# Head norms broadcast by split float32r products, and the squares of a latent's units added on Pool before one sum over channels

## The chip, the cores and the metric

The kernel runs on one core of a Trainium2 chip. The metric is the device time of one execution in microseconds (us). Engines are named as in the profile: PE is TensorE (PEld its weight loads), DVE VectorE, ACT ScalarE, POOL GpSimd, SP SyncE, which here issues most of the DMAs.

## What is computed

Two transformer-like blocks on one sequence of 1024 tokens with 1024 channels, in float32. The first block is a pooling and state-space mixer with a SwiGLU feed-forward part. The second has a latent attention (MLA) branch and an RWKV-7 branch side by side, gates for both, a feed-forward part and a gated extra input. The change touches two places of the second block. In the reference they are:

```python
h = rmsnorm_2(x, g_mix)
z = h @ w_in
z_mla, z_rwkv, z_gate = jnp.split(z, [MLA_COLS, MLA_COLS + RWKV_COLS], axis=-1)
...
c_q, c_kv, k_pe = jnp.split(z_mla, [384, 640], axis=-1)
q = rmsnorm_2(c_q, g_q_a) @ w_uq
kv = rmsnorm_2(c_kv, g_kv_a) @ w_ukv
...
kk = kk / jnp.maximum(jnp.linalg.norm(kk, axis=-1, keepdims=True), 1e-12)
y = wkv7_scan(r, decay, k, v, -kk, kk * a)
y = (y - mean) * lax.rsqrt(var + GN_EPS)
```

The two latents c_q (384 channels) and c_kv (256 channels) are normalized per token over their channels. In the RWKV branch kk and y are normalized per token over each head's 64 channels; there are 8 heads.

## The kernel before

Channels lie on the 128 partitions and tokens along the free axis. A projection is made in units of 128 output channels: `unit_t` takes a unit's weights (`weights`: a DMA into `wr`, a copy on ACT to `wh`, line 103, and a subtraction on DVE to `wl`, line 104, which split the weights into a high and a low float32r part) and makes 48 matmuls of 128x512 into one two-bank PSUM tile `big`: 8 channel blocks of the normed input `hn`, two halves of the tokens, and three products each (`mm3`, lines 139 to 141). Every matmul of a projection reads `hn`, which sets these matmuls apart in the trace. During the RWKV and attention part PSUM holds two `big`, two `chain` and two `ps` tiles.

`rwkv` first works through the recurrence in four blocks of 256 tokens. For a block i it interleaves three generators: `wkv_prep` (elementwise work on DVE and ACT, then small products that fill the tiles `uv`, `bt`, `at`), `wkv_inverse` (a triangular inverse on DVE in 31 steps, lines 1144 and 1145, between DMA round trips through DRAM: `dg` out and in before it, `dg` and `t11` out and in behind it, lines 1119, 1137, 1147 to 1159) and `wkv_chain` (four links of matmuls, lines 1193 to 1210, each with short copies on ACT and DVE between them and the new state at lines 1212 and 1213). A link reads the state that the link before it left. `wkv_out` normalizes a block's output. Both `wkv_prep` and `wkv_out` call `head_rnorm`, 8 times in all: sums over a head's channels by matmul (line 1011), square root on ACT (1013), maximum and reciprocal on DVE (1014, 1015), and then four float32 matmuls (line 1021) that spread the result, which sits in 2 of 32 rows per channel block, over the 64 channels of each head.

Only behind all four blocks does the program text come to `projections`: 5 units of the two latents, then 16 units of the gates, 21 units or 1008 matmuls on `hn`. For each unit of a latent, ACT copies the PSUM tile out (line 1246, then a DMA to `cl`), squares it (line 1248), and PE sums the squares over the channels by 8 matmuls with a column of ones, token block by token block, into the same PSUM tile (line 1250). DVE copies or adds the 8 columns into `ss` (1253, 1255). After the five units `rsqrt` makes the inverse norms of both latents.

The order of the instructions on each engine is not that of the text. A scheduler of the tile framework moves instructions of each engine ahead where their inputs and buffers are free, and freezes the order when the kernel is built; on the chip each engine works through its list in order. So the projections' matmuls, late in the text, can stand between those of the recurrence. What holds an instruction back is its inputs and its tile's buffer. Buffers are handed out in the order of the text: `slot` takes from one ring of 38 buffers of 1040 columns (tag S), which the recurrence uses throughout; `zo` is a ring of two; `wr`, `wh` and `wl` are rings of two.

```python
def slot(self, name, dt=F32, cols=1024):
    t = self.sp.tile([P, self.SC], dt, tag="S", name=self.nm(name), bufs=self.NS)
...
def zo(self, cols=T):
    return self.wp.tile([P, T + 1], F32, tag="zo", name=self.nm("zo"), bufs=2)[:, 0:cols]
```

Of the kernel before, what the change touches and what calls it, by code (L numbers as in the profile page):

```python
# [9 lines left out]
F32 = mybir.dt.float32  # L10
F32R = mybir.dt.float32r
I32 = mybir.dt.int32
AF = mybir.ActivationFunctionType
ALU = mybir.AluOpType
PSUM = bass.MemoryType.PSUM

P = 128
# [31 lines left out]
class Kernel:  # L49
    def __init__(self, ctx, tc, a):  # L50
        self.tc, self.nc, self.a = tc, tc.nc, a
        nc = self.nc
        self.n = 0
        ent = ctx.enter_context
        self.cp = ent(tc.tile_pool(name="cp", bufs=1))
        self.sp = ent(tc.tile_pool(name="sp", bufs=1))
        self.wp = ent(tc.tile_pool(name="wp", bufs=2))
        self.tp = ent(tc.tile_pool(name="tp", bufs=2))
        self.dp = ent(tc.tile_pool(name="dp", bufs=1, space=bass.MemoryType.DRAM))
        self.NS, self.SC = 38, 1040  # L60
        self.cst = self.cp.tile([P, a["cst"].shape[1]], F32, name="cst")
        self.vec = self.cp.tile([P, NVEC], F32, name="vec")
        self.ident = self.cst[:, 0:128]

# [485 lines left out]
    def block1_mixer(self):  # L550
# [9 lines left out]
        def first_weights():  # L560
            w = [pool_w(0), pool_w(1)]
            for i in range(4, 8):
                (nc.sync, nc.scalar)[i % 2].dma_start(xs[i], a["x"][i * P:(i + 1) * P, :])
            nc.scalar.dma_start(self.cst[:, P:], a["cst"][:, P:])
            return w
        pu = self.norm_units(norm_half, xv, first_weights)
        self.wpl = self.slot("wpl")
# [386 lines left out]
    def rwkv(self, hn):  # L954
        nc, a = self.nc, self.a

        self.dg = self.dp.tile([4, 2, 2, 2, 2, 4, 32, 32], F32, name="dg_wkv")
        self.t11 = self.dp.tile([4, 2, 2, 2, 4, 32, 32], F32, name="t11_wkv")
        self.ybd = self.dp.tile([4, P, T], F32, name="ybd")
        self.oka = self.cp.tile([P, 4], F32, name="oka")  # L960
        nc.vector.tensor_scalar(self.oka, self.vec[:, VOFF["k_a_2"]:VOFF["k_a_2"] + 4], -1.0, 1.0, ALU.mult, ALU.add)
        self.rmask = self.cp.tile([P, 256], F32, name="rmask")
        nc.gpsimd.memset(self.rmask, 1.0)
        nc.gpsimd.memset(self.rmask[:, 0:256:64], 0.0)
        s = self.cp.tile([P, 4, 64], F32, name="wkv_s0")
        nc.gpsimd.memset(s, 0.0)
        self.state = s
        step = lambda g: next(g, None)
        live = [[] for _ in range(4)]
        none = iter(())  # L970
        inv = none
        for i in range(5):
            prep = self.wkv_prep(i, live[i]) if i < 4 else none
            step(prep)
            step(inv)
            chain = self.wkv_chain(live[i - 1]) if i else none
            step(chain)
            step(prep)
            step(chain)
            step(prep)  # L980
            step(inv)
            step(chain)
            step(chain)
            if i < 4:
                inv = self.wkv_inverse(i, live[i])
                step(inv)
            if i:
                self.wkv_out(i - 1, live[i - 1])
        return self.attention(*self.latents(*self.projections(hn)))
# [16 lines left out]
    def head_rnorm(self, x, scale, bias, floor):  # L1006
# [6 lines left out]
        nc.scalar.activation(n, ps[:, 0:256], AF.Sqrt, scale=scale, bias=bias)  # L1013
        nc.vector.tensor_scalar(n, n, floor, None, ALU.max)
        nc.vector.reciprocal(n, n)
        out = []
        for i in range(2):
            ps = self.ps()
            for j in range(2):
                c = 904 + (2 * i + j) * P  # L1020
                nc.tensor.matmul(ps[:, j * 256:j * 256 + 256], lhsT=self.cst[:, c:c + P], rhs=n, start=True, stop=True)  # L1021
            out.append(ps)
        return out

# [211 lines left out]
    def projections(self, hn):  # L1236
# [2 lines left out]
        nc, a = self.nc, self.a  # L1239
        cl = self.dp.tile([5, P, T], F32, name="cl")  # L1240
        ss = self.tiny(16, tag="ss16", bufs=1)
        for j, (o, n, g) in enumerate(self.LATENTS):
            for i in range(n):
                ps = self.unit_t(self.weights(a["w_latent"][o + i]), hn)
                c, sq = self.zo(), self.zo()
                nc.scalar.copy(c, ps)
                nc.sync.dma_start(cl[o + i], c)
                nc.scalar.activation(sq, ps, AF.Square, scale=(n * P) ** -0.5)
                for t in range(8):
                    nc.tensor.matmul(ps[:, t:t + 1], lhsT=sq[:, t * P:(t + 1) * P], rhs=self.cst[:, 260:261], start=True, stop=True)  # L1250
                s = ss[:, 8 * j:8 * j + 8]
                if i == 0:
                    nc.vector.tensor_copy(s, ps[:, 0:8])
                else:
                    nc.vector.tensor_tensor(s, s, ps[:, 0:8], ALU.add)
        rs = self.rsqrt(ss, 16, 1.0, EPS)
        self.gd = self.dp.tile([16, P, T], F32, name="gd")
        for u in range(16):
            ps = self.unit_t(self.weights(a["w_gates"][u]), hn)
            g = self.zo()  # L1260
            nc.scalar.activation(g, ps, AF.Sigmoid)
            nc.sync.dma_start(self.gd[u], g)
            if u == 3:
                ps = self.big()
                nc.tensor.transpose(ps[0:16, 0:P], rs, self.ident)
# [235 lines left out]
```

## Time and profile before

| what | value |
|---|---|
| device time, median of 3 runs | 3022.22 us (3017.02 to 3025.08) |
| the profiled execution, its own time | 3025.18 us |
| its span in the trace | 3023.3 us |
| PE busy | 2899.8 us, 96% |
| DVE, ACT, POOL busy | 1404.1, 825.3, 21.8 us |
| mean granted TensorE clock | 0.978 of full speed |

The span is what the profile's rows cover; the execution's own time is 1.9 us longer. A busy share on PE includes each matmul's pipelined tail, so that a stretch of short matmuls looks fuller than it is. A row of a view of stretches gives the stretch and its length, the busy time (and instructions) of PE, PEld, DVE, ACT and, where all are shown, POOL, then the granted TensorE clock as a share of full speed, the DMA share and GB/s. A row of waits gives the instruction and what released it, the total in us, how often, and the longest. A timeline row gives start, length, engine, instruction and, in brackets, the idle time before it. A group row gives line, engine, operation, tiles as out<-in, shapes and count, then the busy time, the mean duration in ns, and the idle time of the engine just before them with what ended it.

### The profile page before, as it was taken

What the parts mean: (1) busy time and instruction counts of PE and PEld (TensorE: products, weight loads), DVE (VectorE), ACT (ScalarE), POOL (GpSimd) and SP (SyncE); (2) the same over time, 40 slices, a digit from 0 to 9 for tenths busy, and PEclk for the clock granted to TensorE, in tenths of its full rate; (3) what the DMA queues carried; (4) which work ended last, traced back from release to release, by engine and by line L of the source; (5) the groups of instructions that cost most, each with busy time, mean ns of one, the idle gap of its engine ahead of it and who ended that gap; (6) DMA issues with size and microseconds to landing.
All of it is one profiled execution on the core that took longest, in us unless ns stands there. A gap on an engine that the chain in (4) does not pass through costs nothing.

```text
span 3023.3 us, 36716 instructions
## 1 busy us (share of the span) xinstructions
PE 2899.8 (96%) x15289; PEld 2327.6 (77%) x15289; DVE 1404.1 (46%) x2469; ACT 825.3 (27%) x1229; POOL 21.8 (1%) x73
## 2 busy tenths in 40 slices
PE   8989999999999999989788999999999999999998
PEld 6777888888888877867566777777888888888877
DVE  7774422222222462276676436545453333333366
ACT  4242311211121344143342334432131221111142
POOL 0000000000000000000000000000000000000000
PEclk9999999999999998999899999999999999999999
DMA  3344111111111234233232320023211111111122
GB/s 133 105 128 146 35 42 42 63 44 40 42 63 49 73 137 153 105 117 90 69 90 88 98 83 13 29 105 134 75 35 42 42 56 49 56 49 42 42 77 98
DMA packets 126390, 225.37 MB, mean 75 GB/s; under 512 B 52177, under 2 KB 73297, under 8 KB 126225
## 3 DMA queue, kind: packets, MB, share of 16 engines
q1 hardware_dynamic: 117200, 211.00, 21.0%
q10 hardware_dynamic: 9024, 12.04, 1.5%
q8 instruction: 120, 1.97, 0.3%
q14 instruction: 46, 0.37, 0.0%
HBM read 171.48 MB, written 48.23 MB: 73 GB/s over the span
## 4 chain that ended last, share of the span: by engine, by line
PE 87%; DVE 9%; issue 2%; ACT 1%; DMA 1%; ACTq 0%; SPq 0%; DVEq 0%
PE big L139 24%; PE big L140 24%; PE big L141 24%; PE big L822 2%; PE chain L855 2%; DVE tt L1145 2%; DVE wt L1144 2%; PE ps L839 1%; PE ps L1114 1%; PE ps L1021 1%; PE big L192 1%; PE chain L1205 0%; PE chain L139 0%; PE chain L140 0%; PE chain L141 0%
## 5 line engine op out<-in xcount | busy, mean ns | idle before, releaser
L139 PE MATMUL big<-hn,wh 128*128 128x512 f32 x1872 | 745.6, 399 | 8.5 <-DVE zo L914 4.0
L141 PE MATMUL big<-hn,wl 128*128 128x512 f32 x1872 | 742.5, 397 | 5.3 <-DVE wl L104 5.2
L140 PE MATMUL big<-hn,wh 128*128 128x512 f32 x1872 | 744.5, 398 | 1.9 <-DVE hn L197 1.9
L139 PEld LDWEIGHTS big<-hn,wh 128*128 128x128 f32 x1872 | 352.8, 189 | 94.2 <-issue 6.2
L141 PEld LDWEIGHTS big<-hn,wl 128*128 128x128 f32 x1872 | 353.4, 189 | 90.7 <-DVE wl L104 8.4
L140 PEld LDWEIGHTS big<-hn,wh 128*128 128x128 f32 x1872 | 353.0, 189 | 88.0 <-issue 3.2
L103 ACT CAST wh<-wr 128x1024 fp32r<-128x1024 f32 (+1 forms) x142 | 141.9, 1000 | 966.4 <-PE big L140 777.4
L104 DVE TENSOR_TENSOR wl<-wr,wh 128x1024 fp32r<-128x1024 f32 (+1 forms) x142 | 165.0, 1162 | 410.5 <-ACT wh L103 405.7
L140 PE MATMUL big<-wk,a 128*128 128x512 f32 x864 | 338.4, 394 | 0.0
L141 PE MATMUL big<-wk,a 128*128 128x512 f32 x864 | 338.3, 393 | 0.0
L139 PE MATMUL big<-wk,a 128*128 128x512 f32 x864 | 334.9, 396 | 1.8 <-ACT wk L103 1.8
L659 DVE TENSOR_TENSOR r<-big,r 128x1024 f32<-128x1024 f32 x144 | 176.2, 1224 | 318.2 <-PE big L141 318.1
L139 PEld LDWEIGHTS big<-wk,a 128*128 128x128 f32 x864 | 160.9, 188 | 43.8 <-ACT wk L103 7.6
L140 PEld LDWEIGHTS big<-wk,a 128*128 128x128 f32 x864 | 162.2, 188 | 38.8 <-DVE wk L104 0.7
L141 PEld LDWEIGHTS big<-wk,a 128*128 128x128 f32 x864 | 162.2, 188 | 37.6
L674 ACT ACTIVATE zo<-big 128x1024 f32<-128x1024 f32 x32 | 32.8, 1026 | 371.4 <-PE big L141 371.4
L668 DVE TENSOR_TENSOR zo<-zo,big 128x1024 f32<-128x1024 f32 x22 | 26.9, 1221 | 205.2 <-PE big L141 205.2
L104 DVE TENSOR_TENSOR wk<-wr,wk 128x1024 fp32r<-128x1024 f32 (+1 forms) x86 | 100.3, 1171 | 31.1 <-ACT wk L103 31.0
L140 PE MATMUL big<-wk,mx 128*128 128x512 f32 x256 | 102.3, 399 | 1.3 <-DVE wk L104 1.3
L139 PE MATMUL big<-wk,mx 128*128 128x512 f32 x256 | 101.0, 401 | 2.3 <-ACT wk L103 2.3
L141 PE MATMUL big<-wk,mx 128*128 128x512 f32 x256 | 101.6, 397 | 0.0
L675 DVE TENSOR_TENSOR zo<-zo 128x1024 f32<-128x1024 f32 x32 | 39.2, 1225 | 131.7 <-ACT zo L674 131.7
(411 smaller groups left out, 3629.5 us busy)
## 6 DMA issues: line engine op xcount, KB each, us to landing
wr<-in_w_ffn_up_dram SPq DMA_DIRECT2D x32, 512.0 KB, 3.2
wr<-in_w_ffn_down_dram SPq DMA_DIRECT2D x32, 512.0 KB, 3.2
zr<-zo SPq DMA_DIRECT2D x24, 512.0 KB, 3.5
wr<-in_w_gate_dram SPq DMA_DIRECT2D x22, 512.0 KB, 3.3
wr<-in_w_up_dram SPq DMA_DIRECT2D x22, 512.0 KB, 3.2
wr<-in_w_down_dram SPq DMA_DIRECT2D x22, 512.0 KB, 3.2
wr<-in_w_gates_dram SPq DMA_DIRECT2D x16, 512.0 KB, 4.9
gd<-zo SPq DMA_DIRECT2D x16, 512.0 KB, 3.0
```

The costliest lines, as they stand in the source:

```text
L103: nc.scalar.copy(hi, x)
L104: nc.vector.tensor_tensor(lo, x, hi.bitcast(F32), ALU.subtract)
L139: nc.tensor.matmul(ps, lhsT=w[0], rhs=x[0], start=start, stop=False)
L140: nc.tensor.matmul(ps, lhsT=w[0], rhs=x[1], start=False, stop=False)
L141: nc.tensor.matmul(ps, lhsT=w[1], rhs=x[0], start=False, stop=stop)
L659: nc.vector.tensor_tensor(res[t], ps, res[t], ALU.add)
L674: nc.scalar.activation(s, ps, AF.Relu)
L675: nc.vector.tensor_tensor(s, s, s, ALU.mult)
L822: nc.tensor.matmul(sc[:, c:c + m], lhsT=qs[e][:, i * P:(i + 1) * P], rhs=ks[e][:, c:c + m], start=True, stop=True)
L855: nc.tensor.matmul(o, lhsT=pts[t // 4][:, (t % 4) * P:(t % 4 + 1) * P], rhs=vh, start=t == 0, stop=t == i)
L1144: nc.vector.tensor_tensor(t3, d[h, j:j + 1, j + 1:32].to_broadcast([64, n, m]), tt[h, 0:n, j:j + 1].to_broadcast([64, n, m]), ALU.mult)
L1145: nc.vector.tensor_tensor(tt[h, 0:n, j + 1:32], tt[h, 0:n, j + 1:32], t3, ALU.add)
```

## The change

`head_rnorm` splits the reciprocal `n` into a high and a low float32r part (a copy on ACT and a subtraction on DVE, into a tile `rh` of the ring of slots), and spreads both with 8 float32r matmuls in place of 4 float32 ones. The selection matrix moves from the constants into a float32r tile `sel`, loaded through a slot and copied on ACT once. In `projections` each latent gets a slot `sq`. Its first unit's squares go straight into `sq`; those of the others go into a `zo` and are added to `sq` on Pool. Once per latent, behind the next unit's matmuls, 8 matmuls sum `sq` over the channels into a `ps` tile, and DVE copies the 8 columns into `ss`. `rsqrt` comes after the first gate unit.

```diff
--- before.py
+++ after.py
@@ -58,7 +58,8 @@
         self.tp = ent(tc.tile_pool(name="tp", bufs=2))
         self.dp = ent(tc.tile_pool(name="dp", bufs=1, space=bass.MemoryType.DRAM))
         self.NS, self.SC = 38, 1040
-        self.cst = self.cp.tile([P, a["cst"].shape[1]], F32, name="cst")
+        self.cst = self.cp.tile([P, 904], F32, name="cst")
+        self.sel = self.cp.tile([P, 512], F32R, name="sel")
         self.vec = self.cp.tile([P, NVEC], F32, name="vec")
         self.ident = self.cst[:, 0:128]
 
@@ -561,7 +562,7 @@
             w = [pool_w(0), pool_w(1)]
             for i in range(4, 8):
                 (nc.sync, nc.scalar)[i % 2].dma_start(xs[i], a["x"][i * P:(i + 1) * P, :])
-            nc.scalar.dma_start(self.cst[:, P:], a["cst"][:, P:])
+            nc.scalar.dma_start(self.cst[:, P:], a["cst"][:, P:904])
             return w
         pu = self.norm_units(norm_half, xv, first_weights)
         self.wpl = self.slot("wpl")
@@ -957,6 +958,9 @@
         self.dg = self.dp.tile([4, 2, 2, 2, 2, 4, 32, 32], F32, name="dg_wkv")
         self.t11 = self.dp.tile([4, 2, 2, 2, 4, 32, 32], F32, name="t11_wkv")
         self.ybd = self.dp.tile([4, P, T], F32, name="ybd")
+        raw = self.slot("sel", cols=512)
+        nc.sync.dma_start(raw, a["cst"][:, 904:1416])
+        nc.scalar.copy(self.sel, raw)
         self.oka = self.cp.tile([P, 4], F32, name="oka")
         nc.vector.tensor_scalar(self.oka, self.vec[:, VOFF["k_a_2"]:VOFF["k_a_2"] + 4], -1.0, 1.0, ALU.mult, ALU.add)
         self.rmask = self.cp.tile([P, 256], F32, name="rmask")
@@ -1013,12 +1017,17 @@
         nc.scalar.activation(n, ps[:, 0:256], AF.Sqrt, scale=scale, bias=bias)
         nc.vector.tensor_scalar(n, n, floor, None, ALU.max)
         nc.vector.reciprocal(n, n)
+        h = self.slot("rh", F32R)
+        hi, lo = h[:, 0:256], h[:, 256:512]
+        self.split(n, hi, lo)
         out = []
         for i in range(2):
             ps = self.ps()
             for j in range(2):
-                c = 904 + (2 * i + j) * P
-                nc.tensor.matmul(ps[:, j * 256:j * 256 + 256], lhsT=self.cst[:, c:c + P], rhs=n, start=True, stop=True)
+                c = (2 * i + j) * P
+                o = ps[:, j * 256:j * 256 + 256]
+                nc.tensor.matmul(o, lhsT=self.sel[:, c:c + P], rhs=hi, start=True, stop=False)
+                nc.tensor.matmul(o, lhsT=self.sel[:, c:c + P], rhs=lo, start=False, stop=True)
             out.append(ps)
         return out
 
@@ -1239,27 +1248,35 @@
         nc, a = self.nc, self.a
         cl = self.dp.tile([5, P, T], F32, name="cl")
         ss = self.tiny(16, tag="ss16", bufs=1)
+        def total(j, sq):
+            ps = self.ps()
+            for t in range(8):
+                nc.tensor.matmul(ps[:, t:t + 1], lhsT=sq[:, t * P:(t + 1) * P], rhs=self.cst[:, 260:261], start=True, stop=True)
+            nc.vector.tensor_copy(ss[:, 8 * j:8 * j + 8], ps[:, 0:8])
+        later = []
         for j, (o, n, g) in enumerate(self.LATENTS):
+            sq = self.slot("sq")
             for i in range(n):
                 ps = self.unit_t(self.weights(a["w_latent"][o + i]), hn)
-                c, sq = self.zo(), self.zo()
+                while later:
+                    total(*later.pop())
+                c = self.zo()
                 nc.scalar.copy(c, ps)
                 nc.sync.dma_start(cl[o + i], c)
-                nc.scalar.activation(sq, ps, AF.Square, scale=(n * P) ** -0.5)
-                for t in range(8):
-                    nc.tensor.matmul(ps[:, t:t + 1], lhsT=sq[:, t * P:(t + 1) * P], rhs=self.cst[:, 260:261], start=True, stop=True)
-                s = ss[:, 8 * j:8 * j + 8]
-                if i == 0:
-                    nc.vector.tensor_copy(s, ps[:, 0:8])
-                else:
-                    nc.vector.tensor_tensor(s, s, ps[:, 0:8], ALU.add)
-        rs = self.rsqrt(ss, 16, 1.0, EPS)
+                s = self.zo() if i else sq
+                nc.scalar.activation(s, ps, AF.Square, scale=(n * P) ** -0.5)
+                if i:
+                    nc.gpsimd.tensor_tensor(sq, sq, s, ALU.add)
+            later.append((j, sq))
         self.gd = self.dp.tile([16, P, T], F32, name="gd")
         for u in range(16):
             ps = self.unit_t(self.weights(a["w_gates"][u]), hn)
             g = self.zo()
             nc.scalar.activation(g, ps, AF.Sigmoid)
             nc.sync.dma_start(self.gd[u], g)
+            if u == 0:
+                total(*later.pop())
+                rs = self.rsqrt(ss, 16, 1.0, EPS)
             if u == 3:
                 ps = self.big()
                 nc.tensor.transpose(ps[0:16, 0:P], rs, self.ident)
```

Lines of the changed file from `wkv_prep` to `wkv_out` are 9 higher than before: 1148 becomes 1157, 1176 becomes 1185, 1201 becomes 1210, 1205 to 1210 become 1214 to 1219, 1212 and 1213 become 1221 and 1222. The lines of the split (103, 104) and of `mm3` (139 to 141) become 104, 105 and 140 to 142.

**On ACT, the squares of the latents.** Before, the second unit of the first latent: its copy and its square follow the cast of its weights (an `L1246`, an `L1248`), and the next unit's cast comes next.

```order
L103 CAST wh_11216<-wr_11214 128x1024
L1246 COPY zo_11131<-big_11082 128x1024
L1248 ACTIVATE zo_11132<-big_11082 128x1024
L103 CAST wh_11285<-wr_11283 128x1024
L1246 COPY zo_11200<-big_11151 128x1024
```

Now the square of the first unit of the first latent, tile `sq_11136` out of the PSUM tile `big_11143`, stands here, behind the last link of the fourth block and the last head norm:

```order
L1211 COPY uv_10359<-chain_11059 64x4x64
L1223 COPY tt_10586<-chain_11070 128x4x64
L1234 ACTIVATE ysq_11101<-tt_10586 128x1024
L1017 ACTIVATE rn_11108<-ps_11103,cst 128x256
L104 CAST rh_11112<-rn_11108 128x256
L1267 ACTIVATE sq_11136<-big_11143 128x1024
```

The square has moved behind the whole recurrence. The copy of that same PSUM tile, `zo_11192<-big_11143`, still stands 134 rows further ahead. The squares of the second and third unit stand ahead too, in the two `zo` buffers.

**On PE, the last link of the fourth block.** Before, matmuls of a gate unit on `hn` stand between the matmuls of the link:

```order
L1199 MATMUL chain_11006<-xs_11004,at_10365 64x64 x8
L140 MATMUL big_12091<-hn_7101,wh_12087 128x512
L141 MATMUL big_12091<-hn_7101,wl_12088 128x512
L139 MATMUL big_12149<-hn_6980,wh_12145 128x512
L1205 MATMUL chain_11017<-uv_10313,bt_10335 64x64
L140 MATMUL big_12149<-hn_6980,wh_12145 128x512
L141 MATMUL big_12149<-hn_6980,wl_12146 128x512
L139 MATMUL big_12149<-hn_6981,wh_12145 128x512
L140 MATMUL big_12149<-hn_6981,wh_12145 128x512
L1205 MATMUL chain_11017<-uv_10313,bt_10335 64x64 x7
L1208 MATMUL chain_11017<-at_10365,uv_10313 64x64 x8
L1210 MATMUL chain_11017<-ar_10056,wst_10983 64x64 x8
```

Now the link's matmuls follow one another and the head norm:

```order
L1208 MATMUL chain_11059<-xs_11057,at_10411 64x64 x8
L1214 MATMUL chain_11070<-uv_10359,bt_10381 64x64 x8
L1217 MATMUL chain_11070<-at_10411,uv_10359 64x64 x8
L1219 MATMUL chain_11070<-ar_10102,wst_11036 64x64 x8
L1015 MATMUL ps_11103<-ysq_11101,cst 32x256 x4
L1029 MATMUL ps_11115<-rh_11112,sel 128x256
```

Seven more rows of lines 1029 and 1030 follow, and only then the next matmuls on `hn`:

```order
L1030 MATMUL ps_11120<-rh_11112,sel 128x256
L140 MATMUL big_11394<-hn_6981,wh_11390 128x512
L141 MATMUL big_11394<-hn_6981,wh_11390 128x512
L142 MATMUL big_11394<-hn_6981,wl_11391 128x512
L140 MATMUL big_11394<-hn_6982,wh_11390 128x512
L141 MATMUL big_11394<-hn_6982,wh_11390 128x512
```

Counted over the lists, of the 1008 matmuls of the 21 units before, 194 stand ahead of the second block's line 1002 (behind that block's head norm), 654 between there and the last matmul of line 1021, and 160 behind it. Now 192 (four units) stand ahead of that line, none between there and the last matmul of line 1030, and 816 (17 units) behind it. The latents' sums over channels (now line 1254) stand among these: 8 behind the first 8 matmuls on `hn`, 8 behind 88 more.

**On DVE, behind the inverse of the second block** (`tt` is its result, its column copy the last work of the inverse). Before, elementwise work for the third block follows (lines 1066, 1069, 1081), with small steps of `rsqrt`; one weight split comes next and then the copies of line 1176 and 1201 that belong to the second block's chain:

```order
L1148 COPY tt_9094<-tt_9094 128x512
L1066 TENSOR_TENSOR ar_9332<-kk_9298,P_9292 128x4x2x64
L1066 TENSOR_TENSOR ar_9333<-kk_9298,P_9292 128x4x2x64
L1069 TENSOR_TENSOR ar_9333<-r_9330,P_9292 128x4x2x64
L160 SCALAR_TENSOR_TENSOR t_11430<-t_11427,t_11423 128x16
L157 TENSOR_TENSOR t_11432<-t_11430,t_11425 128x16
L158 TENSOR_TENSOR t_11432<-t_11432,t_11430 128x16
L160 SCALAR_TENSOR_TENSOR t_11435<-t_11432,t_11430 128x16
L157 TENSOR_TENSOR t_11437<-t_11435,t_11425 128x16
L158 TENSOR_TENSOR t_11437<-t_11437,t_11435 128x16
L160 SCALAR_TENSOR_TENSOR t_11440<-t_11437,t_11435 128x16
L1081 TENSOR_TENSOR r_9330<-r_9330,km_9299 128x1024
```

Now the head norm of the third block comes there, then at once the copies and the new state of the chain's first link (lines 1185, 1210, 1221, 1222). The elementwise work stands behind them, and so do lines 1065 and 1066 of the change (1056 and 1057 before):

```order
L1157 COPY tt_9112<-tt_9112 128x512
L1080 COPY dP_9370<-P_9317 128x16
L1018 TENSOR_SCALAR rn_9335<-rn_9335 128x256
L1019 RECIPROCAL rn_9335<-rn_9335 128x256
L105 TENSOR_TENSOR rh_9339<-rn_9335,rh_9339 128x256
L1062 TENSOR_TENSOR kk_9323<-kk_9323,ps_9342 128x512
L1062 TENSOR_TENSOR kk_9323<-kk_9323,ps_9347 128x512
L1185 COPY at_8792<-chain_9396 32x4x32 x2
L1210 COPY uv_8757<-chain_9454 64x4x64
L1185 COPY at_8809<-chain_9396 32x4x32 x2
L1221 TENSOR_TENSOR wst_9490<-chain_9465,wst_9107 128x256
L1222 TENSOR_TENSOR wst_9490<-wst_9490,dP_8633 128x256
```

## Rows read from the trace of the kernel before

**Rows 1.** Page, part 1.

```profile
PE 2899.8 (96%) x15289; PEld 2327.6 (77%) x15289; DVE 1404.1 (46%) x2469; ACT 825.3 (27%) x1229; POOL 21.8 (1%) x73
```

**Rows 2.** Three stretches, matmuls on hn alone.

```profile
1220.00:1260.00 40.00, 40.00 (x175) 32.45 (x174) 0.00 (x0) 0.00 (x0) 1.00 0.32 118
1380.00:1732.00 352.00, 176.90 (x657) 120.74 (x658) 0.00 (x0) 0.00 (x0) 0.93 0.30 88
1732.00:1770.00 38.00, 36.58 (x159) 29.36 (x157) 0.00 (x0) 0.00 (x0) 1.00 0.30 106
```

**Rows 3.** Seven stretches of the recurrence, all instructions.

```profile
1380.00:1425.00 45.00, 44.93 (x712) 35.24 (x713) 21.28 (x57) 12.53 (x31) 1.14 (x6) 0.96 0.33 93
1425.00:1480.00 55.00, 38.41 (x157) 27.68 (x155) 48.68 (x139) 22.63 (x31) 0.00 (x0) 0.81 0.29 81
1480.00:1524.00 44.00, 43.74 (x633) 34.62 (x633) 20.69 (x40) 14.68 (x30) 1.01 (x5) 1.00 0.30 84
1524.00:1580.00 56.00, 41.33 (x255) 31.30 (x252) 48.77 (x145) 23.61 (x32) 0.13 (x1) 0.91 0.25 68
1580.00:1634.00 54.00, 53.96 (x749) 42.08 (x748) 28.52 (x61) 17.31 (x37) 1.01 (x5) 1.00 0.39 125
1634.00:1682.00 48.00, 35.78 (x151) 27.81 (x150) 37.54 (x119) 11.42 (x14) 0.00 (x0) 0.86 0.24 66
1682.00:1732.00 50.00, 50.00 (x639) 37.41 (x638) 14.36 (x28) 14.41 (x26) 0.00 (x0) 1.00 0.31 101
```

**Rows 4.** The stretches of the chains among these, matmuls on hn alone.

```profile
1380.00:1425.00 45.00, 12.54 (x36) 6.47 (x37) 0.00 (x0) 0.00 (x0) 0.96 0.33 93
...
1480.00:1524.00 44.00, 17.36 (x61) 10.77 (x61) 0.00 (x0) 0.00 (x0) 1.00 0.30 84
...
1580.00:1634.00 54.00, 24.13 (x89) 15.44 (x88) 0.00 (x0) 0.00 (x0) 1.00 0.39 125
...
1682.00:1732.00 50.00, 31.05 (x111) 19.26 (x110) 0.00 (x0) 0.00 (x0) 1.00 0.31 101
```

**Rows 5.** What DVE waited for from 1380 to 1732 us: total us, times, longest.

```profile
DVE wst L1212 <- PE chain L1210: 24.7, 13, 3.0
...
DVE uv L1201 <- PE chain L1199: 17.6, 9, 3.1
```

**Rows 6.** Groups from 1280 to 1735 us: the links' short steps.

```profile
L1201 DVE COPY uv<-chain 64x256 f32<-64x256 f32 x16 | 6.8, 428 | 17.8 <-PE chain L1199 17.6
...
L1213 DVE TENSOR_TENSOR wst<-wst,dP 128x256 f32<-128x256 f32 x16 | 6.8, 423 | 0.5
...
L1196 ACT COPY xs<-chain 128x256 f32<-128x256 f32 x16 | 6.0, 373 | 20.3 <-PE chain L1194 20.3
L1202 ACT COPY uv<-chain 64x256 f32<-64x256 f32 x16 | 5.8, 365 | 29.4 <-DVE uv L1201 29.4
```

**Rows 7.** Group of the weights' subtraction on DVE from 1380 to 1732 us.

```profile
L104 DVE TENSOR_TENSOR wl<-wr,wh 128x1024 fp32r<-128x1024 f32 x15 | 18.3, 1221 | 25.7 <-ACT wh L103 21.7 <-DMA t_wkv<-tt 4.0
```

**Rows 8.** Timeline of DVE behind the third block's inverse: start, us, instruction, idle before.

```profile
1569.92 0.64 DVE L1148 COPY tt<-tt 128x512 f32<-128x512 f32 x1
...
1586.67 0.60 DVE L1176 COPY at<-chain 32x128 f32<-32x128 f32 x2 [2.95 <-PE chain L1174]
```

**Rows 9.** Stretches of 3 us around a head norm in the second inverse.

```profile
1443.00:1446.00 3.00, 0.00 (x0) 0.00 (x0) 2.66 (x12) 1.33 (x2) 0.00 (x0) 0.89 0.00 0
...
1452.00:1455.00 3.00, 3.00 (x14) 1.56 (x13) 2.53 (x6) 1.32 (x3) 0.00 (x0) 0.50 0.51 149
1455.00:1458.00 3.00, 1.69 (x10) 0.58 (x3) 2.78 (x8) 2.97 (x4) 0.00 (x0) 0.90 0.17 70
```

**Rows 10.** Groups from 1280 to 1735 us: the two places that the change rewrites.

```profile
L1021 PE MATMUL ps<-rn,cst 128*128 128x256 f32 x64 | 24.5, 549 | 43.0 <-DVE rn L1015 43.0
...
L1250 PE MATMUL big<-cst,zo 128*128 128x1 f32 x80 | 10.1, 256 | 2.7 <-ACT zo L1248 2.7
```

**Rows 11.** Group of the whole span: Pool's copies.

```profile
L784 POOL COPY kh<-kpe 64x512 f32<-64x512 f32 x16 | 10.5, 665 | 287.1 <-DMA kpe<-rope 162.2 <-PE ps L839 74.0 <-PE chain L855 50.2
```

## The prediction

> **What bounds the kernel now.** I read part 1 of the page first [rows 1]: PE is busy for 96% of the span, so whatever takes work off PE or leaves PE empty is what counts. Then the order of the instructions, since the change is small in the text and large there. Then the stretches where the order differs, 1380 to 1732 us, once for all instructions and once for the matmuls on `hn` alone, and last DVE's waits, the groups and the clock in them.
>
> In a stretch with nothing but projection work PE takes 40 us for 175 matmuls on `hn`, 0.2286 us each at a granted clock of 1.00 [rows 2]. From 1380 to 1732 us it also makes 657 of them, as fillers between the recurrence's own work [rows 2]. That stretch alternates [rows 3]: in 1425 to 1480, 1524 to 1580 and 1634 to 1682 the inverse keeps DVE busy for 48.7 of 55, 48.8 of 56 and 37.5 of 48 us, and PE has little else than fillers. In the four others the chains run and DVE is at most half busy. There 36, 61, 89 and 111 fillers stand [rows 4], 297 in all, so about 360 lie in the inverses. The recurrence is thus bound by DVE in one half and by the links of the chain, back and forth between PE, ACT and DVE, in the other. The fillers ride along.
>
> **The change, part by part.** *The fillers leave.* The first square of the first latent now writes into a slot of the ring that the recurrence uses, and in the order of ACT it stands behind the last head norm. Until then its PSUM tile and both `zo` buffers stay taken, so no further unit can be made. On PE 816 matmuls on `hn` stand behind the recurrence where 160 stood: 656 x 0.2286 = **+150.0 us**, all of it exposed, as the 160 before ran at 38 us with PE full [rows 2].
>
> *What the recurrence gets back.* Bounds: nothing, or everything that the fillers could cost it, 297 x 0.2286 = 68 us in the chains and the fillers' 15 weight splits on DVE, 18.3 us [rows 7]. Between links PE would wait anyway: a link passes an ACT copy of 0.373, a DVE copy of 0.428, an ACT copy of 0.365 and two DVE steps of 0.42 us, 2.0 us in which its own matmuls can't go on [rows 6]. By the order of the last links some 12 fillers, 2.7 us, stand in each link. The surplus of 0.7 us over 16 links is -11 us. That DVE waits 24.7 us in 13 waits and 17.6 us in 9, 1.9 us each, for these matmuls [rows 5] fits relays and not queues of fillers. Of the 15 splits about five fall into idle time, as the 25.7 us in front of this group say [rows 7]; ten are on DVE's way, 10 x 1.22 = -12 us. Behind an inverse, 16 us pass from line 1148 to the first copy of line 1176 [rows 8]; they are DMAs out and in, and fillers stand on PE in front of the chain's first matmul. I take 2 us off for each of three blocks, -6 us (bounds 0 and -12).
>
> *DVE's order.* Behind an inverse DVE did elementwise work for the next block while the DMAs ran. Now it does a head norm there and then waits at the copies of the chain, and lines 1056 and 1057 come between the first two links: two instructions of 128x1024, 1.22 us each by the nearest row [rows 7], in two blocks, +5 us. The lower bound is 0 (the wait of 16 us is not full either way), the upper one +16, if all elementwise work of two blocks is pushed behind the first link.
>
> *The clock.* Without fillers PE stands still for most of each inverse. In 1443 to 1446 us PE did nothing and the granted clock was 0.89 on its way down; in 1452 to 1455 it was full of work at 0.50, the lower level of 1.2 GHz, and it was back at 0.90 only in the next 3 us [rows 9]. So a restart costs some 3 us of work done in 6. I count six restarts: four chains, and two more where DVE's elementwise work stops PE behind a first link: **+18 us**. The bounds: 0, as fillers ran at the lower level before too (0.81 to 0.91 in the inverses [rows 3]); and +108 us, if the chains' own PE time, (44.9 - 12.5) + (43.7 - 17.4) + (54.0 - 24.1) + (50.0 - 31.1) = 107.6 us [rows 3, 4], all ran at half speed.
>
> The Trainium skill speaks against the change here: TensorE: Matmul & The Clock Gate, HAM oscillation, says that an engine that waits between short runs of matmuls falls back to the lower clock each time, again and again. By that the chains would run slow throughout, the +108 us in place of +18; it is a rival below. The trace agrees on the fall behind an idle stretch [rows 9], while the clock is 0.96 to 1.00 over the chains as they are, with fillers in them [rows 3].
>
> *The head norms.* The 64 passes of line 1021 took 549 ns each [rows 10], 8 passes for a norm. Now there are 8 float32r passes of the same 256 columns; the nearest rows are the 0.2286 us of a float32r matmul of 512 columns [rows 2] and the 549 ns as they are, so a norm saves 0 to 3 us of PE. It pays a copy on ACT (0.373 us, same size [rows 6]) and a subtraction on DVE (0.423 us, the two-input step of that size [rows 6]), with their hand-overs some 1 us. PE waits 43.0 us for the reciprocal in all [rows 10] because DVE takes it up late within the inverse, and that doesn't change. In the four places where DVE waits for the products, -1 and +1 cancel: 0 us (bounds -12 and +8).
>
> *The sums.* Before, 80 passes took 10.1 us and PE waited 2.7 us for squares [rows 10], mostly inside inverses and so free. Now 32 passes, 4 us by the same 256 ns with pipelining unchanged, stand in the exposed end; against those that were on the way before, +2 us. The first sum waits for the square (some 1 us) and two adds on Pool. Pool's only copies of float32 take 0.665 us for 64x512 [rows 11], so 1.33 us for 1024 columns with one input; two inputs cost between that and the double of it. I take 2 us: 1 + 2 x 2 us against eight matmuls of 0.23 and the norm's own products, +2 us (bounds 0 and +6). If this cover were gone, it would still be under 6 us.
>
> The Trainium skill, GPSIMD Engine Reference, section Elementwise, puts a two-input float32 add at about twice VectorE's time; with the 1.22 us above that would be an estimated 2.4 us for an add, and the sum would be 1 us more. No row here shows such an add.
>
> The sum goes from the profiled execution's 3025.2 us, 3.0 above the median of 3022.2: 3025.2 + 150.0 - 11 - 12 - 6 + 5 + 18 + 0 + 2 + 2 = **3173 us**. A measurement of this kernel can tell 0.3%, 9 us, from no change.
>
> **The rivals.** *The recurrence was held up by its fillers.* Then all 68 and 18 us and the 12 us behind the inverses come back and the clock costs little: 3025 + 150 - 98 + 10 = 3087 us. For it: PE reads as full in the chains [rows 3]. Against it: a busy share there contains pipelined tails, and the relays of 2 us a link remain.
>
> *The clock stays low in the chains* (the rule above). +108 in place of +18: 3263 us. For it: rows 9. Against it: in the chains PE's own short matmuls fill 107.6 of 193 us now, and a larger part once the fillers are out.
>
> *The recurrence falls to DVE's own time* (the other side: not slower). DVE is the engine with most work of its own there: 219.8 us, the sum of DVE in rows 3, less 18.3 for the splits and plus some 5, 206 us. If every wait went with the fillers, the stretch would shrink from 352 to 206 us and give back 146 us: 3025 + 150 - 146 + 4 = 3033 us, at the edge of no change. It decides once the stretch is under some 210 us. Against it: relays and DMA round trips, 16 us behind each inverse, are untouched by fillers.
>
> *The fillers stay, as the text alone suggests.* Then only the sums' 10 + 3 us and half of line 1021's 24.5 us could go: 3025 - 25 = 3000 us. It asks for a free slot at the first square. The order on ACT and PE speaks against it, and an engine's list is fixed.
>
> **How the numbers follow.** The forecast, which takes in about 40 us to either side: 0.72. Fillers on the way (3060 to 3125): 0.12. Clock low (3225 to 3290): 0.11. DVE's own time: 0.03, of which 0.02 within 0.3% and 0.01 above. Fillers stay: 0.02, faster. The range of 8 in 10 leaves out the ends of both outer rivals: 3110 to 3240 us. Faster 0.02, the same 0.02, slower 0.96.
>
> **What would show it.** In the profile after: a stretch of some 350 us from the second block's line 1002 with no matmul on `hn`, PE well under half busy in the inverses and the clock at the lower level there; a run of about 187 us behind it, PE full at 1.00, against 38 before; DVE's time between inverses as before; the wait for the first sum of a few us. The forecast is wrong if matmuls on `hn` appear between the chains' links, if the stretch without them is under 300 us, or if the chains show the lower clock throughout.

## The result and the profile after

The changed kernel takes 3186.3 us (median of 4 runs, 3183.6 to 3187.6) against 3023.7 us before: ratio 1.054 (95% interval 1.052 to 1.056). That is inside the range of 3110 to 3240 and 13 us above the forecast. The profiled execution took 3187.3 us, its span is 3185.5 us.

Part 1 of the page after, in answer to [rows 1]:

```profile
PE 2924.7 (92%) x15241; PEld 2362.3 (74%) x15241; DVE 1407.5 (44%) x2474; ACT 816.1 (26%) x1228; POOL 29.3 (1%) x76
```

The matmuls on `hn` alone in stretches of the kernel after, in answer to [rows 2]:

```profile
1220.00:1260.00 40.00, 40.00 (x175) 32.47 (x174) 0.00 (x0) 0.00 (x0) 1.00 0.28 105
1380.00:1732.00 352.00, 1.06 (x5) 0.74 (x4) 0.00 (x0) 0.00 (x0) 0.62 0.18 47
1732.00:1960.00 228.00, 192.05 (x816) 154.47 (x814) 0.00 (x0) 0.00 (x0) 0.97 0.28 95
```

The recurrence has lost its fillers (5 matmuls where 657 were), and 816 stand behind it. The seven stretches of the kernel after with all instructions, in answer to [rows 3]:

```profile
1380.00:1425.00 45.00, 36.11 (x542) 29.31 (x541) 19.16 (x35) 11.72 (x29) 1.01 (x5) 0.76 0.22 57
1425.00:1480.00 55.00, 11.27 (x151) 8.36 (x149) 44.47 (x145) 14.90 (x23) 0.13 (x1) 0.56 0.17 43
1480.00:1524.00 44.00, 34.80 (x489) 28.38 (x490) 22.02 (x39) 12.49 (x31) 1.01 (x5) 0.63 0.22 59
1524.00:1580.00 56.00, 12.18 (x198) 9.70 (x196) 45.24 (x147) 11.76 (x20) 0.13 (x1) 0.64 0.17 45
1580.00:1634.00 54.00, 40.71 (x560) 32.84 (x562) 27.11 (x45) 15.08 (x36) 1.01 (x5) 0.65 0.22 54
1634.00:1682.00 48.00, 9.29 (x140) 7.33 (x134) 39.15 (x137) 5.49 (x11) 0.00 (x0) 0.59 0.15 40
1682.00:1732.00 50.00, 34.80 (x530) 30.02 (x531) 10.96 (x26) 8.96 (x21) 1.43 (x1) 0.50 0.14 33
```

PE is nearly empty in the inverses, and the granted clock is 0.50 to 0.76 throughout. DVE's waits in the same 352 us, in answer to [rows 5], did not shrink with the fillers:

```profile
DVE wst L1221 <- PE chain L1219: 31.2, 11, 3.5
DVE at L1185 <- PE chain L1183: 29.0, 10, 7.8
DVE uv L1210 <- PE chain L1208: 25.9, 13, 3.7
```

So the stretch kept its length. The starts of DVE's 16 state steps (line 1212 before, 1221 after) mark the links. The table is worked out from them: the three steps between the four of a block make a block's links, the three gaps from a block to the next hold the inverses, and the last column runs from the last state step to the first matmul of line 756 (757 after), where attention begins.

| kernel, us | links of blocks 1 to 4 | their sum | gaps | first to last | last to attention |
|---|---|---|---|---|---|
| before | 24.3, 33.6, 40.2, 23.9 | 122.0 | 202.1 | 324.1 | 45.8 |
| after | 35.6, 43.6, 45.5, 27.3 | 152.0 | 172.8 | 324.8 | 206.4 |
| e1, norms alone | 39.4, 43.4, 43.4, 23.1 | 149.3 | 199.8 | 349.1 | 14.6 |
| e2, sums alone | 25.8, 30.7, 46.3, 20.3 | 123.1 | 173.8 | 296.9 | 201.4 |
| e3, own buffer | 36.5, 41.6, 41.5, 21.5 | 141.1 | 192.8 | 333.9 | 158.8 |
| x1, after, early | 21.4, 30.1, 29.2, 26.0 | 106.7 | 184.3 | 291.0 | 205.9 |
| x2, norms, early | 26.4, 30.3, 30.3, 23.8 | 110.8 | 208.8 | 319.6 | 33.5 |
| x3, both, early, 37 slots | 28.5, 31.6, 29.5, 23.4 | 113.0 | 218.8 | 331.8 | 36.3 |
| y1, both, early, 38 slots | 23.7, 30.6, 30.3, 23.9 | 108.5 | 213.3 | 321.8 | 33.5 |
| y3, before, early | 24.5, 29.4, 29.0, 23.0 | 105.9 | 201.5 | 307.4 | 58.5 |
| z1, before, 37 slots | 27.7, 43.5, 44.1, 23.3 | 138.6 | 201.4 | 340.0 | 26.7 |

From before to after the gaps fell by 29.3 us, the links grew by 30.0, and the way to attention grew by 160.6. The first state step stayed at 1398.6 us, and behind the start of attention the spans differ by 0.9 us. The table leaves out the time up to the first state step, which comes 8 to 17 us later than before in e1, x2, x3, y1, y3 and z1. Each row is one profiled execution: those of e2 and e3 are 6 us below their medians, those of y1 and z1 6 and 7 us above, so a difference of a few us between rows is not a reading. Of the two parts, the gain in the gaps came with the sums (e2) and the longer links with the norms (e1).

### The profile page after: what moved, and what is told of

Its sections match the earlier page's. It is cut to its first block, busy times and chain, and to the rows that moved or that the text cites. A ratio compares the mean times of both kernels' runs of the same rounds, so it can differ in the third digit from the quotient of the medians.

```text
span 3185.5 us, 36658 instructions
## 1 busy us (share of the span) xinstructions
PE 2924.7 (92%) x15241; PEld 2362.3 (74%) x15241; DVE 1407.5 (44%) x2474; ACT 816.1 (26%) x1228; POOL 29.3 (1%) x76
## 4 chain that ended last, share of the span: by engine, by line
PE 84%; DVE 10%; ACT 3%; issue 2%; DMA 1%; ACTq 0%; POOL 0%; DVEq 0%; SPq 0%; POOLq 0%
PE big L140 24%; PE big L141 23%; PE big L142 23%; PE big L823 2%; DVE tt L1154 2%; DVE wt L1153 2%; PE chain L856 2%; PE ps L840 1%; PE ps L1123 1%; PE big L193 1%; PE chain L1214 0%; PE chain L1208 0%; PE chain L1203 0%; PE ps L1006 0%; PE chain L1202 0%
## 5 line engine op out<-in xcount | busy, mean ns | idle before, releaser
L669 DVE TENSOR_TENSOR zo<-zo,big 128x1024 f32<-128x1024 f32 x22 | 26.9, 1221 | 205.3 <-PE big L142 205.3
L105 DVE TENSOR_TENSOR wk<-wr,wk 128x1024 fp32r<-128x1024 f32 (+1 forms) x86 | 100.3, 1172 | 33.7 <-ACT wk L104 33.6
L1029 PE MATMUL ps<-rh,sel 128*128 128x256 f32 x32 | 12.2, 430 | 105.6 <-ACT rh L104 105.6
```

Of the source, the lines that this page charges most:

```text
L105: nc.vector.tensor_tensor(lo, x, hi.bitcast(F32), ALU.subtract)
```

## The experiments

**The two parts apart.** e1 is the change without its new `projections`; e2 is the new `projections` in the kernel before.

> The head norms' part of the change alone; the latents' squares go to zo and are summed in the unit's own big, as before. In its order 686 matmuls on hn stand between the first and the last link and 55 behind (before: 623 and 187; after: 0 and 816). Theory (the place of the 656 matmuls is what costs): 132 fewer matmuls behind the recurrence are -30 us, 69 more in front of the first link cost 0 to +16 us, so 2995 to 3015 us and no slowdown at all. Rival (the split norms themselves lengthen the recurrence, by a copy, a subtraction and a hand-over in each of four norms): over 3040 us.

Measured 3036.9 us, ratio 1.0046 (1.0031 to 1.0061): slower by 14 us, though 132 fewer matmuls stand behind. Neither number was met. The recurrence is 25 us longer, all of it in the links, as the rival had it; whether by the norms' own work, which was the rival's reason, or by the order is asked by x1 and x2.

> The sums' part of the change alone, head norms as before. In its order 42 matmuls on hn stand between the first and the last link and 816 behind. Theory: this part alone holds back the fillers, so the time is that of the changed kernel, 3186 us, within 15. Rival (the norms cost or save something of their own): under 3160 or over 3210 us.

Measured 3158.5 us, ratio 1.0446 (1.0430 to 1.0462): the rival's side, by 1.5 us. The sums make 136 us of the 163, and the norms some 28 on top. Without fillers the gaps are 28 us shorter, the links not at all.

What the norms did is in DVE's timeline of block 2, from its first state step to the second. First the kernel after:

```profile
1492.27 0.42 DVE L1221 TENSOR_TENSOR wst<-chain,wst 128x256 f32<-128x256 f32 x1 [2.81 <-PE chain L1219]
...
1493.07 1.28 DVE L1075 TENSOR_TENSOR ar<-kk,P 128x512 f32<-128x512 f32 x2
...
1499.65 1.23 DVE L1065 TENSOR_TENSOR km<-km,k 128x1024 f32<-128x1024 f32 x1 [1.09 <-ACT km L999]
...
1501.93 0.68 DVE L1087 TENSOR_TENSOR bk<-km,sg 64x512 f32<-64x512 f32 x1
...
1507.15 1.23 DVE L1090 TENSOR_TENSOR r<-r,km 128x1024 f32<-128x1024 f32 x1
1508.41 0.42 DVE L1221 TENSOR_TENSOR wst<-chain,wst 128x256 f32<-128x256 f32 x1
```

Then e2, with the head norms as before:

```profile
1473.01 1.23 DVE L1081 TENSOR_TENSOR r<-r,km 128x1024 f32<-128x1024 f32 x1 [1.77 <-ACT r L995]
...
1482.12 0.68 DVE L1077 TENSOR_TENSOR bk<-a,sg 64x512 f32<-64x512 f32 x1
...
1487.35 1.29 DVE L1084 TENSOR_TENSOR bv<-ps,v 128x512 f32<-128x512 f32 x2
1488.55 0.41 DVE L1212 TENSOR_TENSOR wst<-chain,wst 128x256 f32<-128x256 f32 x1
...
1501.25 0.42 DVE L1212 TENSOR_TENSOR wst<-chain,wst 128x256 f32<-128x256 f32 x1 [2.87 <-PE chain L1210]
```

In e2 the elementwise steps of the next block are done before the first state step, many while the DMAs behind the inverse run. In the kernel after all of them, `ar` to `r`, stand between the first and the second state step, which are 16.1 us apart. In the order of PE all 32 masked products that need them (line 1123) follow between the second and the third state step, 21.5 us apart; in e2 16 stand there and 16 in the interval before, 10.9 and 12.7 us.

**What holds the fillers.** e3 gives the sum of squares a buffer of its own; the ring pays for it with one slot. e4 also puts the totals into `big` (the last two lines).

```diff
-        self.NS, self.SC = 38, 1040
+        self.NS, self.SC = 37, 1040
-            sq = self.slot("sq")
+            sq = self.tp.tile([P, T], F32, tag="sqo", name=self.nm("sq"), bufs=1)
...
-            ps = self.ps()
+            ps = self.big()
```

> The changed kernel with the sum of squares in a buffer of its own (the ring has 37 slots instead of 38 to make room). In its order 192 matmuls on hn come back between the links and 576 stand behind, since the tile ps of the first total is still handed out behind the recurrence. Theory (two gates stand one behind the other, and the number of matmuls behind sets the time): 240 x 0.2286 = 55 us less than the changed kernel, 3131 us, within 15. Rival (the slot sq is the only thing that bars the fillers): 3000 to 3025 us.

Measured 3150.7 us, ratio 1.0422 (1.0406 to 1.0439). Two gates it is, and the last column fell by 48 us; but the recurrence became 9 us longer with the fillers back in it and one slot fewer, so the time lies 4.7 us above the range.

> The kernel of the run before with the totals in big as well, so that no tile of the latents comes from a ring of the recurrence. In its order 686 matmuls on hn stand between the links and 55 behind, as in the run with the norms alone. Theory: the whole slowdown goes, 2995 to 3015 us. Rival (Pool's adds, the later totals or the norms cost something on the way): over 3040 us.

Measured 3036.3 us, ratio 1.0048 (1.0031 to 1.0065), as e1. Of the 816 matmuls 55 are left behind the recurrence, and 150 us are back. What remains is what e1 has too.

**The order of DVE's steps.** The first step of each block's preparation is put ahead of all other work when the order is made. x1 does this to the changed kernel, x2 to e1, x3 to e4, y3 to the kernel before.

```diff
-            step(prep)
+            with self.tc.high_priority():
+                step(prep)
```

> The changed kernel, its 816 matmuls on hn behind the recurrence as they are, but the first stage of each block's preparation (loads, head norm, the elementwise steps to bv) is put ahead of all other work where the order of the engines is made. In its order the steps ar, km, al, bk, r and bv stand on DVE in front of the chain's first link again, and the second link has 16 of the masked products instead of 32. Theory (the split norms cost 28 us because they push DVE's elementwise steps and PE's masked products in between the links, not by their own work): links and time fall back to those of the sums alone, 3150 to 3165 us, with the sum of the links near 125 us instead of 152. Rival (the split's own copy, subtraction and products cost it, or the clock does): 3175 us or more, links over 140 us.

Measured 3150.5 us, ratio 1.0424 (1.0410 to 1.0437): at the lower end of what the theory had, with 816 matmuls behind as in the kernel after. The links went further down than the 125 us expected, to 106.7, since the third block, which is long in e2 and before too, became short as well; the gaps grew by 11.5 us. The split norms are in x1 as they are in the kernel after, so the longer links of blocks 1 to 3 come with the order and not with the norms' own work. DVE's timeline of block 2 in x1 has `r` and `bv` ahead of the first state step again, and the next state step 10.7 us later:

```profile
1477.01 1.22 DVE L1091 TENSOR_TENSOR r<-r,km 128x1024 f32<-128x1024 f32 x1
...
1482.06 0.69 DVE L1094 TENSOR_TENSOR bv<-ps,v 128x512 f32<-128x512 f32 x1 [0.95 <-PE ps L1007]
...
1486.30 0.42 DVE L1222 TENSOR_TENSOR wst<-chain,wst 128x256 f32<-128x256 f32 x1 [2.50 <-PE chain L1220]
...
1496.96 0.42 DVE L1222 TENSOR_TENSOR wst<-chain,wst 128x256 f32<-128x256 f32 x1 [2.87 <-PE chain L1220]
```

> The head norms alone (the run with +14 us), with the preparation's first stage put ahead as in the run before. 137 matmuls on hn stand behind the recurrence (before: 187), 31 more ahead of the first link. Theory: first to last link falls from 349 to some 320 us and the time to 3000 to 3020 us, no slower than the kernel before. Rival (the split norms cost by themselves): 3030 us or more.

Measured 3017.8 us, ratio 0.9982 (0.9973 to 0.9991), 5 us under the kernel before and the only run whose interval lies below 1. The norms' cost is gone, though the first state step comes 11 us later than before.

> Both parts of the change, with sq in a buffer of its own, the totals in big, and the preparation's first stage put ahead. 149 matmuls on hn behind the recurrence. Theory: neither of the two costs is left, 3000 to 3020 us; against the run with the norms alone the sums save up to 48 passes, at most 6 us. Rival (Pool's adds and late totals cost on the way): 3030 us or more.

Measured 3035.7 us, ratio 1.0041 (1.0029 to 1.0053): a miss. Two runs ask whether the sums or the missing slot did it. y1 is x3 with 38 slots: the sum stays in the first unit's `zo`. y2 is the sums alone in that form.

```diff
-            sq = self.slot("sq")
+            sq = None
-                s = self.zo() if i else sq
+                s = self.zo()
+                sq = sq if i else s
```

> Both parts of the change with the preparation's first stage put ahead, as in the run x3, but the sum of squares stays in the zo buffer of the latent's first unit, so the ring keeps its 38 slots; totals in big. 137 matmuls on hn behind the recurrence, as in x2. Theory (x3 missed by 15 to 35 us because of its 37 slots, with which loads and preparation start later, not because of the sums): 3010 to 3025 us, within 6 us of x2. Rival (Pool's adds and the late totals cost on the way): 3030 us or more.

Measured 3020.7 us, ratio 0.9996 (0.9987 to 1.0005): no different from the kernel before, within 3 us of x2, as the theory had it.

> The sums' part alone in that form: head norms as before, sum of squares kept in zo, totals in big, 38 slots. 187 matmuls on hn behind the recurrence, just as before. Theory (the sums cost 136 us only by the two rings that they take from): 3010 to 3027 us, no difference from the kernel before or a few us less. Rival: 3035 us or more.

Measured 3028.3 us, ratio 1.0017 (1.0008 to 1.0026), 1.3 us over the range and 6 us above the kernel before. 130 of the 136 us are gone; the deferred sums bring nothing.

> The kernel before with a ring of 37 slots instead of 38 and nothing else, so neither split norms nor Pool sums. In its order DVE's steps ar, km, al, bk and r of the last two prepared blocks stand behind the chain's first link and all 32 masked products in the second link, as they do in the changed kernel; 104 matmuls on hn stand behind the recurrence (before: 187). Theory (one slot fewer gives the same long links as the split norms did, which is the cost that x3 had left): the second and third prepared block's two long links take 35 to 38 us each instead of 24.5 and 32.9, the time is 3025 to 3040 us although 83 matmuls, 19 us, fewer stand behind. Rival (the order on DVE and PE in the links does not matter, only the matmuls behind): 3000 to 3010 us.

Measured 3022.6 us, ratio 0.9996 (0.9986 to 1.0006). The links are as expected (36.3 and 36.9 us in blocks 2 and 3), with no split norm in the kernel. The time is 2.4 us under the theory's range and far from the rival's: 16 us of longer links eat most of the 19 us that fewer matmuls behind were worth, and the first state step comes 8 us later. So one slot fewer is enough for long links. Whether the split norms lengthen them because `rh` takes a slot, too, was not tried. The cost that x3 had left is not this one: x3's links are short, 113.0 us against 110.8 in x2, and its gaps are 10 us longer. That the missing slot made x3's 15 us is argued from y1 alone, which also puts the sum elsewhere; the cause stays open.

> The kernel before with the preparation's first stage put ahead and nothing else. 242 matmuls on hn behind the recurrence, 55 more than before. It tells whether the 5 us that x2 is below the kernel before are the norms' or the order's. Theory (the order's): links 12 us shorter, 55 x 0.2286 = 13 us more behind, so 3015 to 3030 us, and x2 is then the split norms' by at most some 10 us. Rival (the split norms are worth nothing once the order is right): within 3 us of x2's 3018.

Measured 3030.7 us, ratio 1.0026 (1.0015 to 1.0036). Links shorter by 16 us, way to attention longer by 12.7, and the first state step 11 us later: 0.7 us above the range. x2 is 13 us lower, but it also has 105 matmuls fewer behind; what the split norms save by their own work was not separated.

**The clock.** The last block's links hold no other block's preparation, and the same instructions ran in them at both clock levels. The second and third of them, all instructions, before (with 12 and 15 fillers):

```profile
1706.00:1714.80 8.80, 8.80 (x174) 6.68 (x174) 2.45 (x8) 1.87 (x5) 0.00 (x0) 1.00 0.01 4
1714.80:1722.70 7.90, 7.90 (x110) 5.79 (x111) 2.48 (x5) 2.98 (x5) 0.00 (x0) 1.00 0.07 28
```

After, no fillers:

```profile
1704.60:1714.80 10.20, 8.78 (x162) 7.65 (x160) 2.39 (x7) 1.87 (x5) 0.00 (x0) 0.50 0.01 2
1714.80:1723.40 8.60, 6.51 (x94) 5.72 (x94) 1.31 (x4) 1.11 (x3) 0.00 (x0) 0.50 0.01 2
```

e2, no fillers either, with its first link ahead:

```profile
1671.90:1679.00 7.10, 5.16 (x98) 4.60 (x100) 1.28 (x3) 1.11 (x3) 0.00 (x0) 0.76 0.35 116
1679.00:1686.20 7.20, 5.49 (x162) 4.58 (x162) 2.46 (x8) 1.87 (x5) 0.00 (x0) 1.00 0.01 2
1686.20:1692.20 6.00, 3.91 (x94) 3.30 (x94) 1.26 (x4) 1.11 (x3) 0.00 (x0) 1.00 0.01 3
```

Without fillers a link takes 6.0 to 7.2 us at the upper level and 8.6 to 10.2 at the lower: 2.6 and 3.0 us for the clock. The fillers cost 1.6 and 1.9 us a link. x4 adds work in the gaps of these links to the changed kernel; nothing uses its products.

```diff
+            warm = lambda x: [nc.tensor.matmul(wp[:, 0:256], lhsT=self.ident, rhs=x, start=True, stop=True) for wp in ([self.ps()] if nwarm else []) for _ in range(nwarm)]
...
+            warm(xs)
```

> The changed kernel with three float32 products of 128x256 added behind each of the three steps of each link of the last block's chain; they read what the step has just made, nothing uses them, and the order of everything else stays. They make PE work in the gaps of the links. Theory (the last block's links take 8.5, 10.2 and 8.6 us and not 7.1, 7.2 and 6.0 as in the run with the sums alone because the clock was at its lower level in them): the granted clock of that stretch rises from 0.50 to over 0.85 and the three links sum to 20 to 24 us instead of 27.3; the time falls by 3 to 7 us. Rival (the links are bound by the hand-overs, whatever the clock): the clock rises and the three links stay over 26 us. If the clock stays at 0.50, nothing is told apart.

Measured 3185.0 us, ratio 1.0539 (1.0525 to 1.0552), no different from the kernel after. The same two links in x4:

```profile
1708.90:1718.60 9.70, 9.70 (x179) 7.60 (x180) 2.42 (x8) 1.87 (x5) 0.00 (x0) 1.00 0.01 3
1718.60:1726.50 7.90, 7.90 (x115) 6.32 (x116) 1.27 (x3) 1.11 (x3) 0.00 (x0) 1.00 0.01 2
```

The clock rose to 1.00, and the three links still sum to 26.1 us, on the rival's side by 0.1. The added products, in the gaps, took what the clock gave. By itself this does not decide between the two; the rows of e2 against those of the kernel after do, for they have the same work without the products.

## Why the prediction was right, and where it was not

Right: the sign, the size and the main term. That the sum came within 13 us owes something to luck, as two errors of opposite sign below show. The first-order reason, 656 matmuls pushed out of the recurrence because the first square waits for a slot of its ring, is shown by the rows on `hn`, by e4 and by y2. The terms against the traces, in us:

| term | predicted | measured |
|---|---|---|
| matmuls on `hn` behind the recurrence | +150 | +155.5 (192.05 - 36.58) |
| gaps: splits and fillers behind the inverse | -12 - 6 | -28.3 (e2), -29.3 (after) |
| fillers in the links and clock there | -11 + 18 | +1.1 (e2); some +7 more in block 4 of the kernel after |
| DVE's order and the norms | +5 + 0 | some +22 (e2 to after, blocks 1 to 3) |
| sums, Pool and the rest of the way to attention | +4 | +5.1 (160.6 - 155.5), and 0.9 behind |

**The mis-sized terms.** First, *DVE's order*: +5 with an upper bound of 16, and some 22 measured. The prediction counted lines 1056 and 1057 alone, in two blocks. The order moved `ar`, `bk` and `r` too, and the masked products on PE behind them; the links of blocks 1 and 2 grew by 9.8 and 12.9 us from e2 to after, and x1 took them back (its block 4, 26.0 us, it could not). How much of this growth the lower clock made was not separated. That was the step that failed: the rows of the order were read for the instructions named in the change, not for what waits behind them. Second, *what the recurrence gets back* in the gaps was taken at 18 us and is 28 to 29, near its bound of 18.3 + 12; it lies in the gaps, as argued. The two errors are 17 and 11 us and mostly cancel, so that the recurrence kept its length to 0.7 us where 6 less were forecast. Third, 816 matmuls took 0.235 us each and not 0.2286, since the clock was still at 0.50 when they began (0.97 over the whole stretch). The norms' own work was taken at 0, and its products did get cheaper: a product of 256 columns took 494 ns in y3 and 357 and 333 ns in x2.

*The fillers in a link* cost 1.6 to 1.9 us and not the 0.7 taken, but the clock takes more than that back where it stays low: block 4 has links of 27.3 us against 23.9 before.

**The mechanism was incomplete.** The prediction named the slot of `sq`. Behind it stands a second gate, the `ps` tile of the first total, handed out in the text's order as well (e3, e4). For the forecast that changed nothing.

**The sums.** An add on Pool took longer than the 2 us taken; its row in the kernel after, from 1690 to 1790 us:

```profile
L1269 POOL TENSOR_TENSOR sq<-sq,zo 128x1024 f32<-128x1024 f32 x3 | 7.2, 2389 | 125.5 <-ACT sq L1267 109.8 <-ACT zo L1267 15.7
L1254 PE MATMUL ps<-cst,sq 128*128 128x1 f32 x32 | 3.8, 248 | 0.6 <-POOL sq L1269 0.6
```

2.39 us is 1.96 times the 1.22 us of [rows 7]. That is the estimate from the Trainium skill, GPSIMD Engine Reference, section Elementwise, and the trace agrees. PE waited 0.6 us for it, so it did not matter.

**The rivals.** *The recurrence was held up by its fillers* (3087): in part. The gaps gave back 28 us of its 98; the links of e2 are as long in sum as before: block 4, where the clock rose to 1.00, is 3.6 us shorter and block 3 is 6.1 us longer. *DVE's own time* (3033): DVE's busy time fell to 208.1 us, the sum of the seven rows above, near the 206 forecast, but its waits stayed. *The fillers stay*: no. *The clock stays low in the chains* (3263) came true in part: 0.50 over block 4, at 2.6 to 3.0 us a link, not 108 us in all. One of the prediction's own signs against itself, the lower clock throughout the chains, was thus met in block 4 and not in the other three stretches (0.63 to 0.76). The rule behind it (the Trainium skill, TensorE: Matmul & The Clock Gate, HAM oscillation) is stated there for a loop that waits for DMAs between its matmuls. Here the waits within a link are for hand-overs, and the same links had 0.50 in the kernel after and 1.00 in e2, so the rule did not decide between them.

## What to carry to other kernels

Where a framework hands out buffers in the order of the text, a new tile from a ring that an earlier stage uses can hold back what comes behind it until that stage ends, as it did here; give late work its own buffer, or one of its own stage. An edit as small as one slot fewer can move the order of a whole stage (z1), so compare the orders for what stands between the links of the longest chain, and not only for the instructions edited. Here one line of priority was worth 19 us to the norms (e1 to x2), and the change with its two side effects taken out (y1) was no different from the kernel before. But y1 carries the priority too, which by itself cost 8 us (y3), and it has 105 matmuls fewer behind than y3; what the split norms and the sums save by their own work stays open.

## What was not expected of the hardware

The same links, instruction for instruction, stayed at a clock of 0.50 in the kernel after, for all 27.3 us of block 4, and went from 0.76 in the first link to 1.00 in the second in e2. What decided between them was not settled. Work added to raise the clock (x4) raised it, but the three links fell only from 27.3 to 26.1 us; e2, without the added products and at 1.00 in two of the three, took 20.3.
